# A sparse 3x3 convolution on one core: two issuers for the first loads, some transfers in halves of 64 partitions, wider matmuls on zeros

## The chip, the core and the metric

The kernel runs on one core of a Trainium2 chip. The metric is device time in microseconds: the median of several executions. A profile of one execution stands beside it. Its span runs from the program's first instruction to its last and is a little shorter than the measured time.

## The reference

The weights are random with nine of ten set to zero, and the convolution is over 16 images of 64 channels, 64 x 64, with 128 output channels, a 3 x 3 window and zero padding of 1:

```python
def reference(x, weight):                  # x 16,64,64,64  weight 128,64,3,3
    x_pad = np.pad(x, ((0, 0), (0, 0), (pad, pad), (pad, pad)), mode='constant')
    output = np.zeros((batch, c_out, h, w), dtype=np.float32)
    ...
        if weight[co, ci, kh, kw] != 0:
            output[b, co] += weight[co, ci, kh, kw] * x_pad[b, ci, kh:kh+h, kw:kw+w]
    return output
```

The kernel computes it as a dense convolution in bf16 with fp32 sums.

## The kernel before

Two images make a pair: image 2p has its 64 channels on partitions 0 to 63, image 2p+1 on 64 to 127. There are eight pairs. A matmul contracts over 64 channels, so two of them, on the two halves of the TensorE array, serve the two images of a pair. An output image is a tile `o` of 128 output channels by 64 x 64 in fp32, 2 MiB.

The inputs are loaded in two ways. The first 32 rows of pair 0 go in fp32 through SyncE's queue into `x_head` (L62, a buffer of the pool of output tiles, hence shown as `o`), and VectorE and ScalarE cast them to bf16 (L99). Everything else is loaded by GpSimd's queue (L63, L68), which casts to bf16 on the way: the rest of pair 0, pairs 1 to 3 and 24 rows of pair 4 at the start; later loads are issued after the last block of pair 1, 2, 3 and 4. The weights (288 KiB) come first on SyncE's queue, before `x_head` (L60).

The weights are cast in three groups, one for each row of the window, and transposed by matmuls with an identity (L109). Around that, TensorE multiplies zeros: 27 matmuls before the weights are there and 28 between the transposes and the first product (`keep_busy`, L84).

Each pair's image is worked in four blocks of 16 rows. A `twos` block forms the sums of neighbouring rows on GpSimd (L167), multiplies these by the middle row of the window into a shared product, and adds to it, for even and odd rows, two products each with differences of the weights. ScalarE copies the shared product from PSUM (L174), and VectorE adds it to each of the others into `o` (L181). The first block of pair 0 is `direct`: three products for each group of 8 rows, evicted by ScalarE and VectorE (L161, L162). The order of instructions on each engine is that of the program text.

All stores are issued by SyncE. The outputs of pairs 0 to 6 are stored whole, two stores of 2 MiB as each pair ends (L207). The last pair's two outputs are stored in two parts of 32 rows each (L204). Every transfer of the hardware queues signals one of eight completion semaphores, in turn and in program order over SyncE and ScalarE, and a transfer that takes a semaphore up again waits for its former use. Two loads and eighteen stores make twenty, so that the last store signals the fourth semaphore. At the end of the program SyncE waits for all of them, one after another, and then the engines meet in a barrier.

Of the kernel before, what the change touches and what calls it, by code (L numbers as in the profile page):

```python
# [8 lines left out]
FP32 = mybir.dt.float32  # L9
BF16 = mybir.dt.bfloat16  # L10
# [17 lines left out]
def kernel(  # L28
# [6 lines left out]
    nc = tc.nc  # L35
# [5 lines left out]
    HEAD = 32  # L41

    const_pool = ctx.enter_context(tc.tile_pool(name="const", bufs=1))
# [4 lines left out]
    psum_pool = ctx.enter_context(  # L48
        tc.tile_pool(name="psum", bufs=8, space=bass.MemoryType.PSUM)
    )  # L50
# [4 lines left out]
    def pair(p):  # L55
        return x[2 * p : 2 * p + 2].rearrange("n i h w -> (n i) h w")

    xs = [x_pool.tile([128, H, W], BF16, name=f"x{p}") for p in range(NP)]
    w_sb = const_pool.tile([C_OUT, C_IN * KH * KW], FP32, name="w_sb")
    nc.sync.dma_start(out=w_sb, in_=weight.rearrange("o i kh kw -> o (i kh kw)"))  # L60
    x_head = o_pool.tile([128, H, W], FP32, name="o")
    nc.sync.dma_start(out=x_head[:, 0:HEAD, :], in_=pair(0)[:, 0:HEAD, :])  # L62
    nc.gpsimd.dma_start(out=xs[0][:, HEAD:H, :], in_=pair(0)[:, HEAD:H, :])  # L63
    ident = const_pool.tile([128, 128], BF16, name="ident")
    make_identity(nc, ident)
# [1 line left out]
    def load(p, a=0, b=H):  # L67
        nc.gpsimd.dma_start(out=xs[p][:, a:b, :], in_=pair(p)[:, a:b, :])  # L68
# [6 lines left out]
    load(EARLY, 0, CUT)  # L75


    idle_rhs = const_pool.tile([128, 128], BF16, name="idle_rhs")
    nc.vector.memset(idle_rhs, 0.0)  # L79
    idle_ps = psum_pool.tile([128, 128], FP32, name="ps")  # L80

    def keep_busy(n):
        for _ in range(n):
            nc.tensor.matmul(idle_ps, idle_rhs, idle_rhs, start=True, stop=True)  # L84

    keep_busy(27)

# [8 lines left out]
    def cast_x(copy, a, b):  # L98
        copy(out=xs[0][:, a:b, :], in_=x_head[:, a:b, :])  # L99
# [24 lines left out]
    nc.vector.tensor_copy(out=wT[:, G0], in_=ps0)  # L124
    ps2 = transposed(G2)
    nc.scalar.copy(out=wT[:, G2], in_=ps2)
    keep_busy(28)
    cast_x(nc.scalar.copy, 9, 18)
    difference(G01, ps0)
    difference(G21, ps2)  # L130
# [26 lines left out]
    def direct(p, o, r0, rows):  # L157
        ps = product(
            [(xs[p], G1, r0, 1), (xs[p], G0, r0 - 1, 1), (xs[p], G2, r0 + 1, 1)], rows
        )  # L160
        nc.scalar.copy(out=o[0][:, r0 : r0 + rows, :], in_=ps[0])  # L161
        nc.vector.tensor_copy(out=o[1][:, r0 : r0 + rows, :], in_=ps[1])  # L162

    def twos(p, o, r0):
        t0 = r0 // 2
        s = s_pool.tile([128, 8, W], BF16, name="s")
        nc.gpsimd.tensor_tensor(  # L167
            out=s, in0=xs[p][:, r0 : r0 + 16 : 2, :], in1=xs[p][:, r0 + 1 : r0 + 16 : 2, :], op=ADD
        )
        shared = product([(s, G1, 0, 1)], 8)  # L170
        pc = []
        for n in range(2):
            c = p_pool.tile([128, 8, W], FP32, name="pc")
            nc.scalar.copy(out=c, in_=shared[n])  # L174
            pc.append(c)
        even = [(xs[p], G21, r0 + 1, 2), (xs[p], G0, r0 - 1, 2)]
        odd = [(xs[p], G01, r0, 2), (xs[p], G2, r0 + 2, 2)]
        for first, terms in ((r0, even), (r0 + 1, odd)):
            ps = product(terms, 8)
            for n in range(2):  # L180
                nc.vector.tensor_tensor(  # L181
                    out=o[n][:, first : r0 + 16 : 2, :], in0=ps[n], in1=pc[n], op=ADD
                )

    for p in range(NP):
        o = [o_pool.tile([C_OUT, H, W], FP32, name="o") for _ in range(2)]
        last = p == NP - 1
        for blk in range(4):
            r0 = 16 * blk
            if BLOCKS[p][blk] == "T":  # L190
                twos(p, o, r0)


                if p == 1 and blk == 3:
                    load(EARLY, CUT, H)
                elif p > 1 and blk == 3 and p + EARLY - 1 < NP:
                    load(p + EARLY - 1)
            else:
                for r, rows in ((r0, 8), (r0 + 8, 8)):
                    direct(p, o, r, rows)  # L200
            if last and blk % 2 == 1:
                for n in range(2):
                    rows = slice(r0 - 16, r0 + 16)
                    nc.sync.dma_start(out=out[2 * p + n][:, rows, :], in_=o[n][:, rows, :])  # L204
        if not last:
            for n in range(2):
                nc.sync.dma_start(out=out[2 * p + n], in_=o[n])  # L207


# [28 lines left out]
```

## Time and profile before

| | |
|---|---|
| time before | 126.42 us, median of 3 (126.32 to 126.64) |
| span of the profiled execution | 124.7 us |
| TensorE matmul busy | 109.0 us, 87% of the span |
| VectorE busy | 82.3 us, 66% |
| GpSimd busy | 41.1 us, 33% |
| ScalarE busy | 39.0 us, 31% |
| granted TensorE clock, mean | 0.959 |
| read from and written to HBM | 17.07 and 33.55 MB |
| weights, from issue to landing | 3.0 us |
| first rows, from issue to landing | 5.6 us |
| a 2 MiB store, from issue to landing (median) | 17.4 us |

Busy shares are averages over the whole span. Below, lines of the page give engine activity in 40 equal slices, the DMA queues with the share of the time of 16 engines that their packets took, and the chain of work that ended last. The rates in GB/s count the bytes that arrive, so a load that casts fp32 to bf16 counts with half of what it reads.

### The profile page before, as it was taken

To read this page: it belongs to the slowest core of one execution; us is meant where nothing else is said; L and a number is where in the kernel's file an instruction comes from. 1 tells how busy PE (TensorE), PEld (TensorE's weight loads), DVE (VectorE), ACT (ScalarE), POOL (GpSimd) and SP (SyncE) were. 2 spreads that over 40 slices of the span, in tenths; PEclk is the share of its full clock that TensorE was granted. 3 is DMA by queue.
4 is the path that set the end of the run, shared out by engine and by line. 5 is a ranking of instruction groups with operands and counts; after the bars stand their busy time and mean duration, and the time that the engine had idled before them with its cause. 6 is when DMAs were issued, how large, how long until landed. Compare 5 with 4: busy or idle time off the path is not lost.

```text
span 124.7 us, 2543 instructions
## 1 busy us (share of the span) xinstructions
PE 109.0 (87%) x1030; PEld 59.5 (48%) x1030; DVE 82.3 (66%) x135; ACT 39.0 (31%) x71; POOL 41.1 (33%) x46
## 2 busy tenths in 40 slices
PE   6999999999999999999999999999999999940000
PEld 6755555555555555555555555555555555510000
DVE  0354777877787778777877787778777878870000
ACT  4545323333333333333333333333333333300000
POOL 6427343533353335333533333333333300000000
PEclk9999999999999999999999999999999999998555
DMA  4999999999999999999999999999999999999991
GB/s 127 356 225 213 215 218 213 211 400 311 350 409 410 318 297 344 436 310 323 302 433 310 318 315 423 420 449 420 426 431 420 436 426 441 415 412 420 428 381 53
DMA packets 4188, 42.93 MB, mean 344 GB/s; under 512 B 464, under 2 KB 464, under 8 KB 976
## 3 DMA queue, kind: packets, MB, share of 16 engines
q1 hardware_dynamic: 2880, 34.90, 66.6%
q0 software_dynamic: 1296, 7.86, 30.8%
q8 instruction: 8, 0.13, 0.4%
q14 instruction: 4, 0.03, 0.1%
HBM read 17.07 MB, written 33.55 MB: 406 GB/s over the span
## 4 chain that ended last, share of the span: by engine, by line
PE 82%; DMA 5%; DVE 1%; issue 1%; DVEq 0%; SPq 0%
PE ps L148 82%; DMA o<-in_x_dram 5%; DVE o L181 1%; DVEq L233 0%; DVE x L99 0%; SPq L60 0%; DVEq L181 0%
## 5 line engine op out<-in xcount | busy, mean ns | idle before, releaser
L181 DVE TENSOR_TENSOR o<-ps,pc 128x512 f32<-128x512 f32 x124 | 77.8, 686 | 22.1 <-PE ps L148 19.8
L148 PE MATMUL ps<-x,wT 64*128 64x504 bf16 (+3 forms) x780 | 88.7, 373 | 0.3 <-DVE x L99 0.3
L148 PEld LDWEIGHTS <-wT 64*128 64x128 bf16 x966 | 54.4, 94 | 48.9 <-issue 0.3
L167 POOL TENSOR_TENSOR s<-x 128x512 bf16<-128x512 bf16 x31 | 35.6, 1151 | 57.5 <-PE ps L148 43.2
L174 ACT COPY pc<-ps 128x512 f32<-128x512 f32 x62 | 33.3, 589 | 64.0 <-issue 61.8
L148 PE MATMUL ps<-s,wT 64*128 64x512 bf16 (+1 forms) x186 | 25.7, 377 | 0.0
L84 PE MATMUL ps<-idle_rhs 128*128 128x128 bf16 x55 | 4.8, 265 | 1.0 <-DVE idle_rhs L79 1.0
L84 PEld LDWEIGHTS <-idle_rhs 128*128 128x128 bf16 x55 | 4.4, 123 | 1.0 <-DVE idle_rhs L79 1.0
L68 POOL DMA_DIRECT2D x<-in_x_dram x8 | 4.4, 561 | 0.0
L103 DVE CAST w_bf<-w_sb 128x192 bf16<-128x192 f32 (+1 forms) x4 | 1.1, 346 | 2.9 <-DMA w_sb<-in_weight_dram 2.9
L162 DVE COPY o<-ps 128x512 f32<-128x512 f32 x2 | 1.4, 692 | 2.0 <-PE ps L148 2.0
L161 ACT COPY o<-ps 128x512 f32<-128x512 f32 x2 | 1.2, 586 | 2.4 <-PE ps L148 2.4
L99 ACT CAST x<-o 128x576 bf16<-128x576 f32 (+1 forms) x2 | 1.5, 804 | 0.8 <-DMA o<-in_x_dram 0.8
L99 DVE CAST x<-o 128x576 bf16<-128x576 f32 x1 | 0.5, 460 | 1.9 <-DMA o<-in_x_dram 1.9
L103 ACT ACT_TABLE_LOAD x1 | 1.3, 1283 | 0.7 <-PEq L222 0.7
L109 PE MATMUL ps<-ident,w_bf 128*128 128x128 bf16 x9 | 1.1, 296 | 0.3 <-DVE w_bf L103 0.3
L103 ACT CAST w_bf<-w_sb 128x64 bf16<-128x64 f32 (+1 forms) x2 | 0.7, 416 | 1.8 <-DMA w_sb<-in_weight_dram 1.8
L109 PEld LDWEIGHTS <-w_bf 128*128 128x128 bf16 x9 | 0.8, 128 | 0.7 <-DVE w_bf L103 0.7
L113 DVE TENSOR_TENSOR wT<-ps,wT 128x384 bf16<-128x384 f32 x2 | 1.0, 548 | 0.0
L63 POOL DMA_DIRECT2D x<-in_x_dram x1 | 0.7, 693 | 0.8 <-POOLq L222 0.8
L79 DVE MEMSET idle_rhs<- 128x64 uint32 x1 | 0.1, 112 | 0.8 <-PEq L222 0.8
L122 ACT CAST wT<-ps 128x384 bf16<-128x384 f32 x1 | 0.5, 480 | 0.4 <-PE ps L109 0.4
(8 smaller groups left out, 2.0 us busy)
## 6 DMA issues: line engine op xcount, KB each, us to landing
out_dram<-o SPq DMA_DIRECT2D x14, 2048.0 KB, 17.4
x<-in_x_dram POOLq DMA_DIRECT2D x6, 1024.0 KB, 15.8
out_dram<-o SPq DMA_DIRECT2D x4, 1024.0 KB, 11.4
o<-in_x_dram SPq DMA_DIRECT2D x1, 1024.0 KB, 5.6
x<-in_x_dram POOLq DMA_DIRECT2D x1, 640.0 KB, 14.0
x<-in_x_dram POOLq DMA_DIRECT2D x1, 512.0 KB, 7.5
x<-in_x_dram POOLq DMA_DIRECT2D x1, 384.0 KB, 24.6
w_sb<-in_weight_dram SPq DMA_DIRECT2D x1, 288.0 KB, 3.0
```

Of the source, the lines that this page charges most:

```text
L68: nc.gpsimd.dma_start(out=xs[p][:, a:b, :], in_=pair(p)[:, a:b, :])
L84: nc.tensor.matmul(idle_ps, idle_rhs, idle_rhs, start=True, stop=True)
L99: copy(out=xs[0][:, a:b, :], in_=x_head[:, a:b, :])
L103: copy(out=w_bf4[:, g, a:b, :], in_=w_v[:, k : k + b - a, :])
L109: nc.tensor.matmul(wps[:, j, :], src, ident, start=True, stop=True)
L113: nc.vector.tensor_tensor(out=wT[:, g], in0=wps, in1=wT[:, G1], op=SUB)
L148: nc.tensor.matmul(ps[n][:, lo:hi, c_lo:c_hi], tap(g, kw, n), src[q, a:b:step, c_lo + kw - 1 : c_hi + kw - 1], start=(i == 0), stop=(i == ...
L161: nc.scalar.copy(out=o[0][:, r0 : r0 + rows, :], in_=ps[0])
L162: nc.vector.tensor_copy(out=o[1][:, r0 : r0 + rows, :], in_=ps[1])
L167: nc.gpsimd.tensor_tensor(out=s, in0=xs[p][:, r0 : r0 + 16 : 2, :], in1=xs[p][:, r0 + 1 : r0 + 16 : 2, :], op=ADD)
L174: nc.scalar.copy(out=c, in_=shared[n])
L181: nc.vector.tensor_tensor(out=o[n][:, first : r0 + 16 : 2, :], in0=ps[n], in1=pc[n], op=ADD)
```

## The change

Three edits are made together. The weights are issued by ScalarE's queue, so that SyncE can issue the first rows at once. The number of hardware transfers grows from twenty to twenty-four, so that the last store signals the eighth completion semaphore, which SyncE checks last: the first rows and three of the outputs are moved as two transfers of 64 partitions each. And the matmuls on zeros are made 512 columns wide, 7 and 7 of them in place of 27 and 28 of 128 columns, for fewer instructions.

```diff
-    nc.sync.dma_start(out=w_sb, in_=weight.rearrange("o i kh kw -> o (i kh kw)"))
+    nc.scalar.dma_start(out=w_sb, in_=weight.rearrange("o i kh kw -> o (i kh kw)"))
     x_head = o_pool.tile([128, H, W], FP32, name="o")
-    nc.sync.dma_start(out=x_head[:, 0:HEAD, :], in_=pair(0)[:, 0:HEAD, :])
+    for q in (slice(0, 64), slice(64, 128)):
+        nc.sync.dma_start(out=x_head[q, 0:HEAD, :], in_=pair(0)[q, 0:HEAD, :])
...
-    idle_rhs = const_pool.tile([128, 128], BF16, name="idle_rhs")
+    idle_rhs = const_pool.tile([128, 512], BF16, name="idle_rhs")
     nc.vector.memset(idle_rhs, 0.0)
-    idle_ps = psum_pool.tile([128, 128], FP32, name="ps")
+    idle_ps = psum_pool.tile([128, 512], FP32, name="ps")
 
     def keep_busy(n):
         for _ in range(n):
-            nc.tensor.matmul(idle_ps, idle_rhs, idle_rhs, start=True, stop=True)
-
-    keep_busy(27)
+            nc.tensor.matmul(idle_ps, idle_rhs[:, 0:128], idle_rhs, start=True, stop=True)
+
+    keep_busy(7)
...
-    keep_busy(28)
+    keep_busy(7)
...
         if not last:
             for n in range(2):
-                nc.sync.dma_start(out=out[2 * p + n], in_=o[n])
+                for q in (slice(0, 64), slice(64, 128)) if 2 * p + n in (2, 3, 5) else (slice(0, 128),):
+                    nc.sync.dma_start(out=out[2 * p + n][q], in_=o[n][q])
```

## The prediction

> **What bounds the kernel now.** I read the page's 40 slices first, then its queue table, then the chain of waits, and last the stretches by window. The slices and the queues:
>
> ```profile
> DMA  4999999999999999999999999999999999999991
> GB/s 127 356 225 213 215 218 213 211 400 311 350 409 410 318 297 344 436 310 323 302 433 310 318 315 423 420 449 420 426 431 420 436 426 441 415 412 420 428 381 53
> q1 hardware_dynamic: 2880, 34.90, 66.6%
> q0 software_dynamic: 1296, 7.86, 30.8%
> ```
>
> All 16 DMA engines are busy from slice 2 to slice 39, and the two queues fill 97.4% of them. The rate only looks uneven. Slices 3 to 8 (213 to 225 GB/s) are GpSimd's cast loads, which read twice the bytes they write; stores alone run at 420 to 440. With s the rate of the stores and c that of the casts' written bytes, s + 2c = about 428 throughout. So the DMA engines are the bound, not TensorE, though the chain reads otherwise:
>
> ```profile
> PE ps L148 82%; DMA o<-in_x_dram 5%; DVE o L181 1%; DVEq L233 0%; DVE x L99 0%; SPq L60 0%; DVEq L181 0%
> ```
>
> The chain ends with the last VectorE sum at 112.0 us; the span ends at 124.7. In between, stores drain. In the tail, with SyncE's waits first and then its semaphore instructions of the last half microsecond:
>
> ```profile
> SPq L233 <- DMA out_dram<-o: 10.4, 4, 3.2
> L233 SPq EVENT_SEMAPHORE  x5: 28/28/28, 123.6 to 123.8; - x5
> ```
>
> SyncE waits 10.4 us for the last four stores, passes the last landing at 123.6, and then checks four more completion semaphores in about 0.24 us. TensorE finishes some 14 us before the end, so its start and its warmth are not on the path unless the store queue runs dry, and the slices show that it never does. What moves the end is the DMA engines' work, their rate, and the 1.1 us after the last landing.
>
> Where stores drain alone and where beside casts is read from stretches (the last column is GB/s, the one before it the DMA share):
>
> ```profile
> core 0: us, PE busy (x) PEld busy (x) DVE busy (x) ACT busy (x) POOL busy (x), PEclk, DMA share, GB/s
> 36.00:40.00 4.00, 4.00 (x40) 2.04 (x37) 3.27 (x6) 1.07 (x2) 1.40 (x2) 1.00 0.98 416
> 40.00:44.00 4.00, 4.00 (x40) 2.13 (x38) 3.27 (x6) 1.07 (x2) 1.15 (x1) 1.00 1.03 332
> 44.00:48.00 4.00, 4.00 (x42) 2.14 (x39) 3.22 (x6) 1.77 (x4) 1.75 (x2) 1.00 1.02 297
> 48.00:52.00 4.00, 4.00 (x42) 2.09 (x39) 2.73 (x5) 1.45 (x3) 2.21 (x3) 1.00 1.01 395
> 52.00:56.00 4.00, 4.00 (x40) 2.09 (x38) 3.27 (x6) 1.07 (x2) 1.16 (x1) 1.00 1.01 344
> 56.00:60.00 4.00, 4.00 (x42) 2.14 (x38) 3.27 (x6) 1.07 (x2) 1.15 (x1) 1.00 1.03 317
> 60.00:64.00 4.00, 4.00 (x42) 2.13 (x38) 3.28 (x6) 1.80 (x4) 2.29 (x3) 1.00 1.00 352
> 64.00:68.00 4.00, 4.00 (x41) 2.04 (x37) 2.68 (x5) 1.42 (x3) 1.67 (x2) 1.00 1.01 362
> ```
>
> [...] The trace of before has no transfer over 64 partitions[...]; it does show 16 engines at 420 to 440 GB/s for 128 partitions, and a rate that falls where two queues share.
>
> **The change part by part.**
>
> 1. *Wide zeros.* 55 matmuls of 128 columns become 14 of 512: 7040 columns against 7168. The first burst took 3.06 us for 27; at the same rate per column 7 wide ones take about 3.1 us. The second took 1.73 us for 28 (5.33 to 7.06); wide it is about 1.8. The first rows reach TensorE at 7.35, so it is hidden. If the array were cold in the second burst, at the first burst's rate, it would end at 8.4 and delay TensorE by 1 us, which 12 us of draining stores hide. The larger memset is VectorE's first, while it waits 2.9 us for the weights. Cost 0.
>
> 2. *Weights on ScalarE.* Issues of 0.38 and 0.43 us now run side by side. The first data came at about 1.75 us, and the first issue still starts at 0.74, so DMA starts no earlier. ScalarE's table load (1.28 us from 0.74) goes behind an issue of 0.4 and ends near 2.4, before the weights land at about 3.8. What can be won is the slow ramp: 88 and 207 GB/s in the half microseconds from 1.5 and 2.0. Against 428 from 1.75 on, 175 KB are missing, 0.4 us. I take 0[...]; both ends, 0 and -0.4, go into the range.
>
> 3. *First rows in halves.* 1.05 MB over 64 partitions at a time. The half rate is the open quantity: either it is full (cost 0) or[...] half of 428, that is 214. In the stretch without casts (1.75 to about 4.9 us) the weights take 0.7 us, and the remaining 2.4 us then move 0.51 MB of rows instead of all; 0.54 MB is put off, worth 1.2 us of all engines. I take +1.2. Beside the casts that follow, the rows [...] lose nothing more. TensorE starts about 2 us later; it is covered by the tail, and the queue of cast loads (until about 25 us) covers the later first store.
>
> 4. *Outputs 2, 3 and 5 in halves.* Six transfers of 1 MB. With s = 2r - 428 from each stretch's rate r, the stores have moved 3.40 MB by 36 us (380, 319 and 368 GB/s from 24 us), then 5.02, 5.96, 6.62, 8.07, 9.11, 9.93, 11.03 and 12.21 MB at the ends of the rows above. At 2.10 MB each, output 2 drains from 38.0 to 46.0 us, output 3 to 53.2, output 4 to 62.0, output 5 to 69.7. No cast shares with them where the rate is about 400 or more: until 40, from about 49 to 52.3, and from about 62.6 to 66. So output 2 is alone for 2.0 us and output 3 for 3.3. With the delay of these two (half of 5.3, 2.65 us) output 5 starts near 64.7 and is alone for 1.3. Half the rate in 6.6 us loses 3.3 us. Beside casts, I take no loss[...]. The other end: [...] a store packet takes twice its time there too, over about 15 us of which half is stores: +7.5.
>
>    SyncE's three more issues cost it 0.3 to 1.3 us each, where it waits up to 20 us for VectorE. The new waits on older completions are met: the row that now needs output 1's completion is issued at 60.2, and output 1 landed at 41.0. Output buffers come free later by some 4 us; output 9 reuses the buffer of output 2 and starts after 60 us, against a landing at 50.2. Hidden.
>
> 5. *Last semaphore.* The last store now signals the one that is checked last; four checks of 0.06 us leave the tail: -0.24. A certain, small gain.
>
> Sum: 1.2 + 3.3 - 0.24 = +4.3 us: 126.42 becomes 130.7.
>
> **The rivals.**
>
> *B, the halves are free.* For it: the casts share much of the time[...]. [...] Then only the tail remains: 126.2, no change that can be measured.
>
> *C, free, and the ramp is filled too.* Two queues at once keep engines busy from 1.75 us, which speaks from the 0.78 DMA share between 2.0 and 2.5 us: 126.42 - 0.24 - 0.4 = 125.8, faster.
>
> *D, the halves lose beside casts too.* 130.7 + 7.5 = 138.2[...]. [...]
>
> **How the numbers follow.** A, the forecast, 0.46; B 0.22; C 0.23; D 0.09. A and D are slower (0.55). B falls within 0.3% (126.04 to 126.80). C counts as faster, and a little of B beside it for part of the ramp, while as much of C falls short of 0.4: faster 0.24, same 0.21. The time is A's, 130.7. The range reaches to just below C (125.7) and up to half of D's extra loss, 135.5; beyond stand a full D and about a tenth in all.
>
> **What would show it.** In the changed profile: A wants stretches without casts near 50 us at 210 to 250 GB/s in place of 418, hardware queue's share of engine time clearly over 66.6%, first rows landing after 8 us (6.8 before), and a last landing near 128. B and C want those stretches at 410 or more. All want SyncE to pass the last landing with no four checks behind it. C wants over 300 GB/s between 2.0 and 2.5 us. A store-alone stretch at full rate during outputs 2 or 3 refutes A outright.

## The result and the profile after

The changed kernel takes 138.4 us (median of 6, 136.1 to 141.4) against 126.5 us before. The ratio is 1.0847, with a 95% interval of 1.0763 to 1.0931: it is slower by about 11 us. The forecast was the right way, slower, but its range ended at 135.5. Three of the six executions took 136.1 to 137.9 us, and the ratio rests on them; the other three were slower, 138.9 to 141.4, and the profile below is of one of these.

The first view of the page after, the slices and the queues, answers to the first lines shown of before. The profiled execution spans 138.4 us, so a slice is 3.5 us:

```profile
DMA  5999999579899999999999999999999999999930
GB/s 156 223 225 222 220 208 207 106 303 379 297 320 330 223 194 253 315 334 256 324 369 275 301 353 341 424 421 440 412 436 436 412 428 445 409 417 426 395 137 28
q1 hardware_dynamic: 2800, 34.60, 65.3%
q0 software_dynamic: 1296, 7.86, 27.6%
q10 hardware_dynamic: 144, 0.29, 0.8%
```

The bytes are the same, so the DMA engines must somewhere have moved less in a microsecond. Three places show: a hole at the eighth slice, with 106 GB/s and a DMA share of 0.5; a low stretch around the fourteenth and fifteenth, at 223 and 194 while the share says busy; and a long end, 137 and 28. The windows (the last two columns are the DMA share and GB/s) put times to them:

```profile
24.00:28.00 4.00, 4.00 (x42) 2.17 (x38) 3.27 (x7) 1.17 (x3) 1.15 (x1) 1.00 0.51 99
28.00:32.00 4.00, 4.00 (x42) 2.15 (x38) 3.06 (x5) 1.91 (x4) 2.50 (x3) 1.00 0.79 328
44.00:48.00 4.00, 4.00 (x42) 2.10 (x38) 2.87 (x5) 1.83 (x4) 1.90 (x2) 1.00 0.99 229
48.00:52.00 4.00, 4.00 (x40) 2.13 (x38) 2.92 (x6) 1.26 (x3) 1.53 (x2) 1.00 0.98 201
128.00:132.00 4.00, 0.00 (x0) 0.00 (x0) 0.00 (x0) 0.00 (x0) 0.00 (x0) 0.50 0.90 379
132.00:136.00 4.00, 0.00 (x0) 0.00 (x0) 0.00 (x0) 0.00 (x0) 0.00 (x0) 0.50 0.24 102
```

The same first two stretches of before:

```profile
24.00:28.00 4.00, 4.00 (x40) 2.10 (x38) 3.27 (x6) 1.07 (x2) 1.14 (x1) 1.00 1.06 380
28.00:32.00 4.00, 4.00 (x42) 2.07 (x38) 3.21 (x6) 1.74 (x4) 1.72 (x2) 1.00 1.00 319
```

From 24 to 28 us the DMA engines of the changed kernel are half idle: the cast loads of the start are done and no store is there yet. From 44 to 48 us, with stores alone, they are fully "busy" and move half of 428 GB/s: the median 16 KB packet that starts there takes 1.26 us, where such a packet took 0.62 us before, and the busy share counts a slow packet like a fast one. From 128 us on the share falls with the rate, to 0.90 and then 0.24; before, the end fell from 393 to 82 GB/s within two microseconds.

The hole comes from a late start of TensorE. The timeline after, from the second burst of zeros to the first product (start and length in us, engine, line, operation, idle time and its releaser in brackets), and below it two lines of before:

```profile
5.53 1.67 PE L85 MATMUL ps<-idle_rhs 128*128 128x512 bf16 x7
11.37 0.46 DVE L100 CAST x<-o 128x576 bf16<-128x576 f32 x1 [6.21 <-DMA o<-in_x_dram]
11.88 5.67 PE L149 MATMUL ps<-x,wT 64*128 64x512 bf16 x36 [4.68 <-DVE x L100]
```

```profile
5.33 1.73 PE L84 MATMUL ps<-idle_rhs 128*128 128x128 bf16 x28
7.35 3.99 PE L148 MATMUL ps<-x,wT 64*128 64x512 bf16 x36 [0.29 <-DVE x L99]
```

The weights are on time, but VectorE waits 6.2 us for the first rows. TensorE starts at 11.88 us where it started at 7.35, and its first 36 matmuls take 5.67 us where they took 3.99, after the array stood idle for 4.7 us; the granted clock reads 0.60 from 11.88 to 13.88 us and 0.54 in the 2 us after that, and it read 1.00 over these 36 before. An array that multiplies more slowly after such a wait is called cold below; `e10` tests this. The first store is issued at 28.0 us; before it was 21.8.

### The profile page after: what moved, and what is told of

Same layout as the page of the kernel before. It is cut to its first block, busy times and chain, and to the rows that moved or that the text cites. A ratio compares the mean times of both kernels' runs of the same rounds, so it can differ in the third digit from the quotient of the medians.

```text
span 138.4 us, 2472 instructions
## 1 busy us (share of the span) xinstructions
PE 110.8 (80%) x989; PEld 58.1 (42%) x989; DVE 82.4 (60%) x135; ACT 39.0 (28%) x71; POOL 41.2 (30%) x46
## 3 DMA queue, kind: packets, MB, share of 16 engines
q1 hardware_dynamic: 2800, 34.60, 65.3%
## 4 chain that ended last, share of the span: by engine, by line
PE 75%; DMA 7%; DVE 1%; issue 1%; DVEq 0%; SPq 0%
PE ps L149 75%; DMA o<-in_x_dram 7%; DVE o L182 1%; DVEq L237 0%; SPq L63 0%; DVE x L100 0%; DVEq L100 0%; DVEq L182 0%
## 5 line engine op out<-in xcount | busy, mean ns | idle before, releaser
L149 PE MATMUL ps<-x,wT 64*128 64x504 bf16 (+3 forms) x780 | 90.5, 379 | 4.7 <-DVE x L100 4.7
L149 PEld LDWEIGHTS <-wT 64*128 64x128 bf16 x966 | 55.8, 95 | 53.9 <-issue 6.8
L85 PE MATMUL ps<-idle_rhs 128*128 128x512 bf16 x14 | 4.8, 505 | 1.2 <-DVE idle_rhs L80 1.2
L85 PEld LDWEIGHTS <-idle_rhs 128*128 128x128 bf16 x14 | 1.5, 119 | 3.2 <-issue 1.4
```

Of the source, the lines that this page charges most:

```text
L85: nc.tensor.matmul(idle_ps, idle_rhs[:, 0:128], idle_rhs, start=True, stop=True)
L149: nc.tensor.matmul(ps[n][:, lo:hi, c_lo:c_hi], tap(g, kw, n), src[q, a:b:step, c_lo + kw - 1 : c_hi + kw - 1], start=(i == 0), stop=(i == ...
```

## The experiments

All times are medians, and differences in us are of medians; the ratio is to the kernel before measured beside it, with its 95% interval.

**First group: which of the splits, and why.** Three kernels vary the splits of the change, and a control keeps the halved stores alone.

`e1`: the change with whole stores; the first rows stay in halves.

```diff
-                for q in (slice(0, 64), slice(64, 128)) if 2 * p + n in (2, 3, 5) else (slice(0, 128),):
-                    nc.sync.dma_start(out=out[2 * p + n][q], in_=o[n][q])
+                nc.sync.dma_start(out=out[2 * p + n], in_=o[n])
```

> The changed kernel with outputs 2, 3 and 5 stored whole; only the first rows stay in halves of 64 partitions. [...] the losses of engine time from 30 us on go, those of the start and of the gap before the first store stay (about 1.5 and 2.5 us): 129.5 to 131. Rival, the stores alone cost everything: 126.3. Rival, the late first rows alone cost everything: about 138.

Measured: 131.65 us, with no interval: three executions took 131.6 to 132.2 us and one 129.18. By the medians, the halved stores thus cost some 6.7 of the 11.9 us, and the first rows with the rest some 5.1; by the fastest execution of each kernel it is 6.9 and 2.9. The second part is therefore known only roughly from this run. Neither rival holds: no part alone does it all.

`e3`: every split by image rows, over all partitions.

```diff
-    for q in (slice(0, 64), slice(64, 128)):
-        nc.sync.dma_start(out=x_head[q, 0:HEAD, :], in_=pair(0)[q, 0:HEAD, :])
+    for r in (slice(0, 16), slice(16, 32)):
+        nc.sync.dma_start(out=x_head[:, r, :], in_=pair(0)[:, r, :])
...
+                for r in (slice(0, 32), slice(32, 64)) if 2 * p + n in (2, 3, 5) else (slice(0, 64),):
+                    nc.sync.dma_start(out=out[2 * p + n][:, r], in_=o[n][:, r])
```

> The changed kernel with every split by image rows over all 128 partitions: as many transfers, sizes and semaphores, other partitions. [...] 126.2 (before, less 0.24 for four checks at the end). Rival, the number or the smaller size of transfers costs the time: 136 to 138 again.

Measured: 129.24 us, ratio 1.0248 (1.0168 to 1.0329). Most of the loss went, yet 2.7 us stayed, which neither theory had. In its trace the weights took 5.7 us to land where they took 3.0. That led to the second group.

`e4` is as `e3` for the first rows, but outputs 2, 3 and 5 leave in two transfers of 64 partitions, both from partitions 32 to 95. Of these three outputs it leaves out half of the channels and stores the others twice, which changes no count and no size. `e5` is the same with the halves of the change.

```diff
+                    src = slice(32, 96) if 2 * p + n in (2, 3, 5) else q
-                    nc.sync.dma_start(out=out[2 * p + n][q], in_=o[n][q])
+                    nc.sync.dma_start(out=out[2 * p + n][q], in_=o[n][src])
```

> Head by rows; outputs 2, 3 and 5 in two transfers of 64 partitions that both read partitions 32 to 95 (half of the outputs' channels are written from the wrong partitions; bytes, counts and destinations are those of the halves). [...] 126.2 as by rows, and no hardware packet of 16 KB takes 1.2 us. Rival, 64 partitions are slow whichever they are: as the next run, 131 to 135.

> Head by rows, outputs 2, 3 and 5 in halves 0 to 63 and 64 to 127 as in the change. [...] the start and the gap before the first store as before, the stores' losses stay (5 to 7 us, and 2 for engines that end apart): 131 to 135. Rival, the late first rows cost everything: 126.3.

Measured: 129.31 us, ratio 1.0234 (1.0207 to 1.0261), for the middle partitions; 135.28 us, 1.0697 (1.0670 to 1.0724), for the halves. Count, size, destination and issue are the same in both, only the partitions differ, and that is worth 6.0 us. The middle partitions cost what whole-width rows cost (129.24). So it isn't 64 partitions that are slow, nor more transfers, but 0 to 63 and 64 to 127. The windows from 40 to 44 us, in both runs almost without casts, first of the middle partitions:

```profile
40.00:44.00 4.00, 4.00 (x40) 1.85 (x38) 3.27 (x7) 1.07 (x2) 1.14 (x1) 1.00 1.14 451
```

and of the halves:

```profile
40.00:44.00 4.00, 4.00 (x40) 1.84 (x38) 3.27 (x7) 1.07 (x2) 1.15 (x1) 1.00 1.14 269
```

The DMA share is 1.14 in both (a packet counts whole where it starts, so a short stretch can pass 1), the rate 451 against 269, and the median 16 KB packet takes 0.61 us against 1.27. The runs show that it matters which partitions are read; for what reason, they do not show.

**Second group: the other parts alone.** Each starts from the kernel before.

`e6`: the wide matmuls on zeros, as in the change, and nothing else.

```diff
...
-            nc.tensor.matmul(idle_ps, idle_rhs, idle_rhs, start=True, stop=True)
+            nc.tensor.matmul(idle_ps, idle_rhs[:, 0:128], idle_rhs, start=True, stop=True)
...
-    keep_busy(27)
+    keep_busy(7)
...
-    keep_busy(28)
+    keep_busy(7)
```

> The kernel before with the wide matmuls on zeros alone. Theory: hidden, since the first rows land after the second burst: 126.4. Rival, wide matmuls warm the array less well or end later, and the first store comes late: 127 or more.

Measured: 126.62 us, ratio 1.0008 (0.9986 to 1.0030). They cost nothing that can be measured.

`e7`: the weights on ScalarE's queue.

```diff
-    nc.sync.dma_start(out=w_sb, in_=weight.rearrange("o i kh kw -> o (i kh kw)"))
+    nc.scalar.dma_start(out=w_sb, in_=weight.rearrange("o i kh kw -> o (i kh kw)"))
```

> The kernel before with the weights issued by ScalarE and all else as it was; first rows whole. By rows the weights landed at 6.4 us and not 3.8, beside rows that had full rate. Theory of shared turns: here too the weights are late (after 5.5 us), the first product starts after 9 us, cast loads run dry before the first store: 127.5 to 129. Rival, only the split of the rows made the weights late: 126.0 to 126.5.

Measured: 129.57 us, ratio 1.0225 (1.0179 to 1.0271). One word costs 3 us. Its timeline:

```profile
7.01 1.15 DVE L103 CAST w_bf<-w_sb 128x192 bf16<-128x192 f32 x4 [6.08 <-DMA w_sb<-in_weight_dram]
8.58 3.01 PE L84 MATMUL ps<-idle_rhs 128*128 128x128 bf16 x28
11.53 1.82 PE L148 MATMUL ps<-x,wT 64*128 64x512 bf16 x16
```

The weights' cast starts at 7.0 us (3.8 before), when the first rows have landed too (6.1 us after their issue at 0.7). The second burst of zeros then runs on an array that stood idle, at 3.01 us for 28 where it took 1.73, and it now stands between the weights and the first product, which starts at 11.5. On one queue the weights went ahead: in the trace of before, between 3 and 5 us, 94 row packets and the last 9 weight packets start. On two queues 77 row packets and 73 weight packets start in those 2 us, so the two loads go about one packet for one, as the theory of shared turns has it. The 128 weight packets (93 ns each) are eight for each of the 16 engines; if each of the eight waits for a row packet of 309 ns, they take 8 x 402 ns = 3.2 us in place of 0.7. This is an estimate from this trace's packets, and it covers 2.5 of the 3.3 us by which the landing moved (6.3 us after issue against 3.0); the rest stays open.

`e8`: the last store on the last semaphore, by splitting outputs 2 to 5 by rows.

```diff
-                nc.sync.dma_start(out=out[2 * p + n], in_=o[n])
+                for r in (slice(0, 32), slice(32, 64)) if 2 * p + n in (2, 3, 4, 5) else (slice(0, 64),):
+                    nc.sync.dma_start(out=out[2 * p + n][:, r], in_=o[n][:, r])
```

> The kernel before with outputs 2 to 5 in two transfers of 32 rows over all partitions, so that the last of 24 transfers signals the semaphore checked last; nothing else. Theory: 126.2, the four checks of 0.06 us are gone and nothing is lost. Rival, smaller stores lose engine time (by rows 34 to 54 us lost some 0.6 us): 126.5 to 127.

Measured: 126.92 us, ratio 1.0028 (1.0008 to 1.0049). The split takes more than the checks gave.

`e9`: outputs 10, 11 and 12 in halves, where no load shares the engines.

```diff
-                nc.sync.dma_start(out=out[2 * p + n], in_=o[n])
+                for q in (slice(0, 64), slice(64, 128)) if 2 * p + n in (10, 11, 12) else (slice(0, 128),):
+                    nc.sync.dma_start(out=out[2 * p + n][q], in_=o[n][q])
```

> The kernel before with outputs 10, 11 and 12 in halves of 64 partitions, where no load shares the engines. [...] halves alone run at half of 428 GB/s: 6.29 MB take 29.4 us in place of 14.7, so 126.4 + 14.7 = 141[...]: 133 to 141, with stretches near 214 GB/s and packets of 1.2 us. Rival, two queues are needed for the loss: 126.4.

Measured: 138.17 us, ratio 1.0886 (1.0825 to 1.0947). Some of its windows, with stores alone:

```profile
88.00:92.00 4.00, 4.00 (x40) 1.95 (x38) 3.27 (x6) 1.07 (x2) 1.15 (x1) 1.00 1.00 426
96.00:100.00 4.00, 4.00 (x42) 2.02 (x40) 2.69 (x6) 1.72 (x4) 1.98 (x2) 1.00 0.98 287
112.00:116.00 4.00, 0.00 (x0) 0.00 (x0) 0.18 (x1) 0.00 (x0) 0.00 (x0) 0.95 1.00 199
120.00:124.00 4.00, 0.00 (x0) 0.00 (x0) 0.00 (x0) 0.00 (x0) 0.00 (x0) 0.50 1.02 430
128.00:132.00 4.00, 0.00 (x0) 0.00 (x0) 0.00 (x0) 0.00 (x0) 0.00 (x0) 0.50 0.55 231
132.00:136.00 4.00, 0.00 (x0) 0.00 (x0) 0.00 (x0) 0.00 (x0) 0.00 (x0) 0.50 0.17 72
```

Halves lose without any load beside them: from 92 to 116 us the stretches of 4 us move 199 to 336 GB/s, against 426. Most of them pass the 214 that was expected of halves alone; why they do, the trace doesn't show. What it shows besides is a long end: from 128 us on, the share falls to 0.55 and 0.17 and the rate to 231 and 72 GB/s, over 8 us.

**Third group: why a late start costs the end.** `e10` and `e13` start from `e7`, `e11` and `e12` from the kernel before.

`e10`: the first burst is long enough to bridge the wait for the late weights.

```diff
-    keep_busy(27)
+    keep_busy(78)
```

> The kernel before with the weights on ScalarE (129.57 us) and 78 instead of 27 matmuls in the first burst of zeros, so that TensorE does not idle from 4.1 to 7.6 us while it waits for the late weights. Theory, a cold array is part of the delay: the second burst takes 1.7 us and not 3.0, the first store comes 1.3 us or more earlier, the gap between loads and stores shrinks by as much: 127.7 to 128.5. Rival, only the late weights count: 129.6.

Measured: 127.99 us, ratio 1.0113 (1.0095 to 1.0131). The timeline has the second burst short again, and the first product 1.5 us earlier:

```profile
8.35 1.73 PE L84 MATMUL ps<-idle_rhs 128*128 128x128 bf16 x28
10.01 3.98 PE L148 MATMUL ps<-x,wT 64*128 64x512 bf16 x36
```

So 1.6 of the 3 us were a cold array.

`e11`: the last store on the last semaphore through four loads of 1 KB.

```diff
+    tiny = const_pool.tile([16, 4, 16], FP32, name="tiny")
+    for i in range(4):
+        nc.sync.dma_start(out=tiny[:, i, :], in_=pair(0)[0:16, i, 0:16])
```

> The kernel before with four more loads of 16 partitions by 64 bytes behind the first rows, into a tile that nothing reads; twenty-four transfers, so the last store signals the semaphore checked last, and no store is split. Theory: 126.2 to 126.3, the 0.24 us of four checks less the small loads. Rival, the checks are not worth their count, or the small loads cost as much: 126.5.

Measured: 126.36 us (22 executions), ratio 0.9993 (0.9984 to 1.0002): not told from no change. The four checks are gone from the trace's end, and the profiled span is 124.5 us against 124.7.

`e12`: the weights stay on SyncE and the first rows go to ScalarE.

```diff
-    nc.sync.dma_start(out=x_head[:, 0:HEAD, :], in_=pair(0)[:, 0:HEAD, :])
+    nc.scalar.dma_start(out=x_head[:, 0:HEAD, :], in_=pair(0)[:, 0:HEAD, :])
```

> The kernel before with the first rows issued by ScalarE and the weights by SyncE. Theory of turns ([...] eight weight packets of 93 ns wait for eight row packets of 309 ns): weights late as with the queues the other way round, 128.5 to 130. Rival, ScalarE's queue is served later than SyncE's: weights on time, 126.4.

Measured: 129.55 us, ratio 1.0227 (1.0208 to 1.0246), with the weights landing after 5.7 us. Which engine issues hardly matters (129.55 us, and 129.57 in `e7`); what matters is that the whole rows and the weights go out on two queues at once.

`e13`: more rows loaded ahead.

```diff
-    EARLY, CUT = 4, 24
+    EARLY, CUT = 4, 56
```

> The kernel before with the weights on ScalarE (129.57 us) and 56 rows of pair 4 loaded at the start in place of 24. Theory, the time is lost because cast loads run dry before the first store: 1.05 MB more to read fills 2.4 us of the gap: 127.0 to 127.8. Rival, the time is lost elsewhere (TensorE is the bound of the rest): 129.6.

Measured: 129.81 us, ratio 1.0260 (1.0246 to 1.0273). The theory missed. Its windows:

```profile
24.00:28.00 4.00, 4.00 (x42) 1.88 (x40) 2.68 (x6) 1.72 (x4) 1.99 (x3) 1.00 0.99 233
36.00:40.00 4.00, 4.00 (x42) 1.80 (x40) 3.27 (x6) 1.54 (x3) 1.51 (x2) 1.00 0.65 275
```

The hole at 24 us is closed, and another stands at 36 to 40, where in `e7` the share was 1.03: what was loaded early is missing there.

**Fourth group: where the hole goes.**

`e14` is `e7` with all loads one pair further ahead; `e15` is `e11` with the same edit.

```diff
-    EARLY, CUT = 4, 24
+    EARLY, CUT = 5, 24
```

> The kernel before with the weights on ScalarE (129.57 us) and all loads one pair further ahead: pairs 1 to 4 and 24 rows of pair 5 at the start. With 56 rows of pair 4 the gap before the first store closed but another opened at 39 us, since less was left to load then. Theory, engines run dry because first stores come late while too little is left to load: with a whole pair more ahead both gaps close, 126.9 to 127.6. Rival, a late TensorE costs its delay whatever is loaded: 129.5.

> The kernel before with the four small loads (126.36 us) and all loads one pair further ahead. The kernel before loses 0.5 us of engine time between 22 and 26 us. Theory, that goes too: 125.9 to 126.2. Rival, longer queues of loads hold back stores and the last store ends no earlier: 126.4 or more.

Measured: `e14` 128.36 us, ratio 1.0148 (1.0116 to 1.0179), between both theories. The DMA engines are full from 24 us until the loads are over, and then:

```profile
96.00:100.00 4.00, 4.00 (x40) 1.77 (x38) 3.27 (x7) 1.07 (x2) 1.15 (x1) 1.00 1.00 418
100.00:104.00 4.00, 4.00 (x40) 1.84 (x38) 3.14 (x6) 1.85 (x4) 1.83 (x2) 1.00 0.46 193
104.00:108.00 4.00, 4.00 (x40) 1.84 (x38) 2.82 (x5) 1.37 (x3) 0.48 (x1) 1.00 1.09 459
```

The store queue runs dry at 100 us, waiting for pair 6, which a TensorE 4.7 us late finishes at 103.9. `e15` took 127.00 us, ratio 1.0036 (1.0023 to 1.0050), slower than `e11`; why loads further ahead cost a little there was not followed up.

`e16`: the kernel before with the first rows in halves alone.

```diff
-    nc.sync.dma_start(out=x_head[:, 0:HEAD, :], in_=pair(0)[:, 0:HEAD, :])
+    for q in (slice(0, 64), slice(64, 128)):
+        nc.sync.dma_start(out=x_head[q, 0:HEAD, :], in_=pair(0)[q, 0:HEAD, :])
```

> The kernel before with the first rows in halves of 64 partitions alone; the weights stay first on SyncE. [...] rows at half rate [...] land at 11 us or later and start TensorE cold, 130 to 132 as with the weights on ScalarE and the rows in halves (131.65). Rival, that loss was the weights': 126.5.

Measured: 132.41 us, ratio 1.0446 (1.0406 to 1.0486), a little over the range expected. The halves land 7.0 and 10.0 us after issue, and TensorE starts at 12.3 us. The hole of the changed kernel is here too, with no other part of the change:

```profile
24.00:28.00 4.00, 4.00 (x42) 2.02 (x40) 3.27 (x6) 1.07 (x2) 1.15 (x1) 1.00 0.53 103
28.00:32.00 4.00, 4.00 (x42) 2.08 (x40) 3.40 (x6) 1.07 (x2) 1.67 (x2) 1.00 0.59 238
```

With the weights on ScalarE beside them (`e1`, 129.2 to 132.2) it is no worse, and the weights land 3.1 us after issue. The loss of `e7` does not come about there: the first packet of the halved rows starts at 2.6 us, 0.9 us after the weights' first, where in `e7` whole rows start at 1.7 us, ahead of the weights. Why the halves start later is open. That the halved rows are slow for the same reason as the halved stores was not tested with rows in partitions 32 to 95; their packets of 8 KB take 0.50 us in the median, and 0.31 before.

## Why the prediction was right in kind and too small

That the DMA engines' work sets the time, and not TensorE's 82% of the chain, was read rightly, except that TensorE's start was taken to be free. The cause named, the author's assumption that halves at partition 64 move at half rate, is shown in kind by `e4` against `e5` (451 and 269 GB/s from 40 to 44 us), though no run shows why; and a stretch at 229 GB/s stood where 210 to 250 was forecast. One sign that was asked for failed: the hardware queue's share of engine time fell to 65.3% in place of rising over 66.6%. By these shares its time on each engine rose from 83 to 90 us, but the span rose more. The sizes taken were too small, by 7.7 us in all (6.4 by the ratio), and one step was wrong.

To see where the time went, the packets of each trace can be added up as engine work: bytes stored plus twice the bytes cast, over 428 GB/s. A kernel's lag is how much less of this work it has done than the kernel before at the same time. All lags below are estimates of this kind.

1. *Wide zeros at nothing*: right (`e6`).
2. *The weights on ScalarE at 0 to -0.4*: wrong in sign, +3 us alone (`e7`). The step looked only at issue time and at the engines' ramp, and assumed that a second issuer changes nothing at the engines, which nothing had shown. It didn't ask who goes first. In the whole change this loss does not come about: the weights land 3.2 us after issue.
3. *The first rows at +1.2*: `e16` has +5.9. The +1.2 itself was nearly right: `e16` lags by 1.5 us at 10 us. "Lose nothing more" beside the casts was not quite so, since row packets of 8 KB still took 0.5 us there, in place of 0.31. But the sentence "it is covered by the tail, and the queue of cast loads (until about 25 us) covers the later first store" is the step that failed. In the changed kernel TensorE came 4.5 us late, where about 2 had been taken, and partly cold; the first store came 6.2 us late, and the DMA engines stood half idle from 24 to 28 us. In `e16` the lag grows from about 1 us at 26 us to 5.8 at 36, and then stays there to the end: the late start costs 4.8 of the 5.9 us.
4. *The stores at +3.3*: +6.0 (`e5` less `e3`) to 6.7 (the change less `e1`). Half rate alone was right in kind (199 to 336 GB/s against 426 in `e9`), and in size for stores alone. In `e5` the 16 KB packets took 4.4 us more of the time of all 16 engines than in `e4`, by an estimate from the packets' durations: 3.0 of it while casts held less than a tenth of the engines (3.3 was forecast), and 1.4 beside more casts, where nothing had been taken. About 1 us more comes at the end, by the same estimate. In the profiled execution of the whole change the DMA share is 0.56 over the last 10 us before the last packet ends (127.1 to 137.1), where it was 0.87 before (113.1 to 123.1).
5. *The last semaphore at -0.24*: `e11` gives -0.16, not told from zero; the trace shows the checks gone.

The full rival D, at 138.2, met the time nearly, but that was luck: it had the whole extra loss beside casts and none from the late start.

The wrong step rests on a reading that is easy to make: that 12 us of stores drain after TensorE, so that TensorE has 12 us of slack. Those are the last outputs' own stores. Slack is what is queued ahead of a store at the thinnest place. Before, the store issued at 98.6 us landed 10.2 us later, of which its own 2.1 MB take 4.9 at 428 GB/s, so at most some 5 us of queue and completion stood before it. At the start it was about 3 us: the first store was issued at 21.8 us, and with no store beside them the cast loads ran dry at about 25 (`e7`). `e10`, `e7` and `e14`, with first stores 2.7, 4.2 and 4.7 us late, cost about 1.5, 3.0 and 1.8 us. The gaps stand in different places: the DMA share is 0.77 from 30 to 32 us in `e10`, 0.55 from 24 to 28 in `e7`, and 0.46 from 100 to 104 in `e14`. Loads ahead (`e14`) close the early thin place and leave the next.

None of these versions is shown to be faster than the kernel before.

## What to carry to other kernels

Where the DMA engines are the bound, don't cut transfers at partition 64: three outputs so cut cost 6.0 us here (`e5` against `e4`). A cut of four outputs along the free dimension cost about 0.4 us (`e8`), and three outputs moved by 64 partitions around the middle took no longer than over all 128 (129.31 and 129.24 us); how a whole output would best be cut into such parts was not tried. A load that others wait for goes first on the same queue as the bulk, since here it landed 3.0 us after issue that way, and after 5.7 to 6.3 with the whole rows on a second queue (`e12`, `e7`). And measure the slack of an engine off the bound at the thinnest point of the queue that it feeds, not by the length of the tail.

## What had not been expected of the hardware

- Partitions 32 to 95 moved as fast as all 128 (129.31 against 129.24 us), where 0 to 63 and 64 to 127 cost 6.0 us more.
- A load of 288 KB took 5.7 us (`e12`) and 6.3 us (`e7`) to land, in place of 3.0, when the whole rows went out on another queue at the same moment, whichever of the two engines issued it.
- The DMA share doesn't show the loss: it reads 0.98 to 1.14 in stretches of 4 us with halves that move 201 to 269 GB/s, and 1.14 in one that moves 451.
- After a wait of 3.5 us (`e7`) 28 matmuls on zeros took 3.01 us, and 1.73 when matmuls filled the wait (`e10`). A wait of 2.6 us did nearly as much in `e4` (2.69 us for 7 wide matmuls in place of 1.67). It is not all that counts: in `e16` 28 of them took 2.51 us with no wait. In `e7` the filler meant to keep the array warm became part of the delay.
